# VectorE takes over GpSimd's arithmetic in a fused S5, GLU and mixture-of-experts layer, and TensorE takes eight modulation rows

## The chip, the cores and the metric

One core of a Trainium2 chip runs one launch of the kernel. The metric is the device time in microseconds, the median of several runs. Engines are named as in the profile: PE is TensorE, DVE is VectorE, ACT is ScalarE, POOL is GpSimd, SP is the engine that issues the transfers.

## The reference

One trunk layer on 1024 latent tokens and 256 context tokens of width 1024, in float32. What matters here, cut down:

```
c -> silu -> w_ada -> shift, scale, gate rows for both sub-layers      (modulation)
h = layer_norm(x) * (1 + scale) + shift
proj = h @ w_in  -> u_a, z_b, gate_b, gate_c, merge_a, merge_b
S5:    32 groups of 16 channels, 64 complex states, forward and backward
       s[t] = ab * s[t-1] + bb @ u[t];  y = Re(c @ s) + d * u
       context first, latent scans start from its final states; then GLU
conv:  conv3(gate_c * z), gated by gate_b, then conv_w_out
mix = (sigmoid(merge_a) * a + sigmoid(merge_b) * b) @ w_o
x1 = layer_norm(ALPHA * x + gate * mix);  h2 = modulate(layer_norm(x1))
router: top-1 expert group of 4, top-2 of its 8 experts; SwiGLU experts
out = layer_norm(ALPHA * x1 + gate2 * moe(h2))
```

## The kernel before, in words

A float32 product runs on TensorE in three passes: each operand is split in a rounded "hi" (ACT, `L91`) and a remainder "lo" (a subtraction, `L92`, on DVE or POOL), and hi·hi, lo·hi and hi·lo are summed in PSUM (`L95`, `L96`, `L97`). The whole program is one stream for each engine in the order in which the Python code emits it; nothing is reordered afterwards. The pieces are interleaved by hand with generators.

Until 129 us the modulation rows of the first sub-layer, the layer norm and the product that gives u are made. **Preparation** (to 290 us) then runs 20 "half units": `half()` issues the eight three-pass products (24 matmuls, tiles `g` from `hh`, `hl`, `wh`, `wl`) of one half of a weight unit of `w_in`; a unit is loaded two ahead (`load_unit`, tile `raw`) and its weight split one ahead (`split_unit`, tiles `wh`, `wl` of 128x1024, `L92` on POOL). The lists `before[h]` and `after[h]` say which piece of the S5 tables is made around half h: for each of four quarters q, `prep_v` makes complex products on DVE (`cmul`, `L692` to `L697`, six operations of 128x512), transposes and splits them; `prep_r` makes two more `cmul`, direction 0 on DVE and direction 1 on POOL, copies `bb` into `bpd` (`L722`), multiplies on PE (`L743`) and splits into `rh`, `rl`, half of it on POOL; `prep_m` makes the last tables. Every second half, `ada_slot` moves the remaining 32 modulation rows on by one stage: load the row's weights (`raw<-in_w_ada`), then on DVE `acc` = the sum over eight blocks of weight times the conditioning scalar (`L780` once, `L782` seven times), then on PE one matmul with a column of ones (`L788`) and on DVE an addition into `mr` (`L790`). One filler of dummy matmuls (`warm`, `L101`) stands in q = 3.

The **in-loop** (to 385 us) runs j from -2 to 15 over 16 pairs of groups: `in_a` transposes u (`L854`) and splits it on DVE (`ul`), `in_b` multiplies (12 matmuls into tiles `t`) and copies the results out of PSUM (`L875` on ACT, `L876` and `L877` on DVE), `in_c` transposes back (`L885`, `L887`) and copies to the scan's buffers (`L895`). A `half()` stands ahead of `in_b` at each odd j, an `ada_slot` at the end of each even j. The **scan** (to 528 us) is 160 steps on DVE (`L901`, `L904`); beside it PE runs the remaining halves, and 19.1 us of filler until the read-out. The read-out follows to 614, then the **GLU** to 752: for each of eight row blocks m, `glu_split` splits the weights on POOL, and `glu_post` multiplies the sigmoid in (`L1069`, POOL) and merges on DVE (`L1070` to `L1072`). The weight w_o (tiles `OW`, eight of 128x1024) is scaled by the gate row g2, three on POOL inside the GLU (`L1167`), five after it (`L1190`), and split with `wo_hi` (ACT) and `wo_lo` (`L1197`, DVE and POOL in turn). The **w_o product** runs in eight tiles of 128 tokens; between the tiles' products `stage_a` forms ALPHA·x + product (`L1451`), `stage_b` normalizes and modulates to `h` (`affine`, a DVE, an ACT and a POOL operation, `L1395`, `L1399`, `L1400`), `stage_c` transposes `h` (`L1504`) and runs the router. `stage_ab(7)` does the same for the last tile. Routing ends at 912 us; the experts take the rest.

Of the kernel before, what the change touches and what calls it, by code (L numbers as in the profile page):

```python
# [49 lines left out]
def block_kernel(ctx: ExitStack, tc: tile.TileContext, I, out):  # L50
# [598 lines left out]
    def half(before=(), after=()):  # L649
# [5 lines left out]
        if n == 0:  # L655
            split_unit(i + 1)
# [24 lines left out]
    def cmul(eng, n, q, tab, d, lo, a, b, c_, d_, op_re, op_im):  # L681
# [9 lines left out]
        x, y = (sb(sp, f"c{n}{z}", full) for z in "xy")  # L691
# [8 lines left out]
    def prep_v(q, d):  # L700
# [71 lines left out]
    def ada_rest(q):  # L772
# [6 lines left out]
        acc = sb(AR["pl"], "acc", [P, P])  # L779
        V.tensor_scalar(acc, w[:, 0, :], sc[:, 0, 0:1], None, op0=ALU.mult)  # L780
        for k in range(1, NK):
            V.scalar_tensor_tensor(acc, w[:, k, :], sc[:, k, 0:1], acc, op0=ALU.mult, op1=ALU.add)  # L782
# [5 lines left out]
        PE.matmul(pb[0:1, 0:P], ones, acc, start=True, stop=True)  # L788
# [27 lines left out]
    for q in range(4):  # L816
# [92 lines left out]
    for j in range(-2, NPAIR):  # L909
# [7 lines left out]
        if j % 2 and j < NPAIR - 1:  # L917
# [25 lines left out]
    while hstep[0] < 49:  # L943
        half([steps(8)])
# [28 lines left out]
    def ro_b(pr):  # L973
# [3 lines left out]
        warm(py, {0: 19.1, 12: 1.3, 13: 4.0, 15: 0.85}.get(pr, 0))  # L977
# [58 lines left out]
    def glu_split(m, xs=(1, 2, 0), eng=G):  # L1036
# [27 lines left out]
    def glu_post(m, n):  # L1064
# [4 lines left out]
        G.tensor_tensor(sgm, sgm, sga, op=ALU.mult)  # L1069
# [69 lines left out]
    ld(g2, mod_d[0].partition_broadcast(P))  # L1139
# [4 lines left out]
    for m in range(NK):  # L1144
# [5 lines left out]
        for n in range(2):  # L1150
# [54 lines left out]
    wo_hi(3)
    wo_scale(4, G)
    wo_hi(4)
    wo_scale(5, V)
    wo_scale(6, G)
    wo_lo(3, V)  # L1210
    wo_hi(5)
    wo_lo(4, G)
    wo_scale(7, V)
    wo_hi(6)
    wo_lo(5, V)
    wo_hi(7)
    wo_lo(6, G)
    wo_lo(7, V)
# [7 lines left out]
    G.memset(xgs[0], 0.0)  # L1226
# [218 lines left out]
    def stage_a(i, fill=()):  # L1445
# [14 lines left out]
    def stage_b(i, fill=()):  # L1460
# [4 lines left out]
        if i < 6:  # L1465
            affine(h2, x1, *o, bc["sc2"], bc["sh2"], G)
# [563 lines left out]
```

## Time and profile before

| | |
|---|---|
| runs shown | 1692.76, 1698.22, 1701.19 us, median 1698.22 |
| profiled execution | 1694.1 us, span 1692.3 us (1.8 us around it) |
| mean granted TensorE clock | 0.987 |
| busy: PE, DVE, ACT, POOL | 1577.4 (93%), 1347.9 (80%), 729.9 (43%), 495.3 us (29%) |

Busy shares say little by themselves, since the stages have different limits: they are read by stage, with the waits of the engine that has almost no idle time there. A "busy" PE includes dummy matmuls and matmuls at the lower clock.

### The profile page before, as it was taken

The page shows a single profiled execution, that of the slowest core. Times are in us where ns is not written, and L with a number is a line of the kernel's source. Part 1 is how long each engine was busy: PE and PEld are TensorE (multiplying, and loading weights), DVE is VectorE, ACT ScalarE, POOL GpSimd, SP SyncE. Part 2 cuts the span into 40 slices and gives each one's busy share as a digit, 9 for nine tenths or more (in the row PEclk, how much of TensorE's full clock was granted, in tenths as well). Part 3 has the DMA queues.
Part 4 walks back from the last instruction along what each step waited for, and adds up shares of the span by engine and source line. Part 5 has one row for each costly group of instructions (what it writes and reads, how often), then busy time and mean ns, then how long its engine had stood idle before and what let it go on. Part 6 is the DMA issues. An engine that isn't in the chain of part 4 may idle for free.

```text
span 1692.3 us, 23483 instructions
## 1 busy us (share of the span) xinstructions
PE 1577.4 (93%) x7594; PEld 1243.1 (73%) x7594; DVE 1347.9 (80%) x2871; ACT 729.9 (43%) x1059; POOL 495.3 (29%) x366
## 2 busy tenths in 40 slices
PE   7899899999998999988998999999999999999984
PEld 3688777888887777766876777777777777777751
DVE  7757987669999548987687695999995999686878
ACT  1443322442212352222222574777764777555632
POOL 1436562012222423444333120121221222120127
PEclk9999999999999999999999999999999999999998
DMA  8415767862322565554544595899995999776872
GB/s 318 160 55 185 215 193 238 275 209 101 100 81 78 157 190 180 192 165 160 185 174 136 192 363 199 327 362 356 373 339 195 353 356 373 288 264 238 292 303 100
DMA packets 141732, 381.62 MB, mean 226 GB/s; under 512 B 17632, under 2 KB 76160, under 8 KB 116992
## 3 DMA queue, kind: packets, MB, share of 16 engines
q1 hardware_dynamic: 130912, 362.80, 61.4%
q0 software_dynamic: 10656, 16.80, 2.7%
q8 instruction: 83, 1.36, 0.3%
q14 instruction: 81, 0.66, 0.1%
HBM read 336.98 MB, written 68.76 MB: 240 GB/s over the span
## 4 chain that ended last, share of the span: by engine, by line
issue 25%; DMA 24%; DVE 23%; PE 18%; POOL 4%; ACT 2%; SPq 2%; POOLq 1%; another core or an unknown queue 1%; DVEq 0%; ACTq 0%
DMA y_d<-yt,tbi 11%; DMA xo<-h_d,tbi 8%; DVE vs L904 4%; DVE sa L901 3%; DVE acc L782 3%; PE g L95 2%; PE g L97 2%; PE g L96 2%; DVE vc L904 1%; PE pu L95 1%; PE pu L97 1%; PE pu L96 1%; DMA raw<-in_w_ada 1%; PE misc L1511 1%; POOL h L1400 1%
## 5 line engine op out<-in xcount | busy, mean ns | idle before, releaser
L92 DVE TENSOR_TENSOR lo<-raw,hi 128x1024 fp32r<-128x1024 f32 x376 | 440.8, 1220 | 30.9 <-ACT hi L91 20.2
L91 ACT ACTIVATE hi<-raw 128x1024 fp32r<-128x1024 f32 x376 | 371.7, 1050 | 33.7 <-PEq L1871 20.5
L1728 POOL DMA_INDIRECT y_d<-yt,tbi x37 | 92.2, 2493 | 381.2 <-DVE yt L1721 300.0
L95 PE MATMUL g<-hh,wh 128*128 128x512 f32 x448 | 178.5, 398 | 0.0
L96 PE MATMUL g<-hl,wh 128*128 128x512 f32 x448 | 175.6, 392 | 0.0
L97 PE MATMUL g<-hh,wl 128*128 128x512 f32 x448 | 175.5, 392 | 0.0
L92 POOL TENSOR_TENSOR wl<-raw,wh 128x1024 fp32r<-128x1024 f32 x27 | 66.4, 2458 | 203.1 <-ACT wh L91 203.1
L95 PE MATMUL y<-hi,hh 128*128 128x512 f32 x256 | 102.5, 400 | 6.1 <-PEq L1871 2.1
L95 PE MATMUL g<-hi,xh 128*128 128x512 f32 x256 | 102.1, 399 | 4.2 <-issue 0.3
L95 PE MATMUL u<-hi,xh 128*128 128x512 f32 x256 | 105.8, 413 | 0.0
L97 PE MATMUL g<-hi,xl 128*128 128x512 f32 x256 | 100.6, 393 | 1.2 <-DVE xl L92 1.2
L97 PE MATMUL u<-hi,xl 128*128 128x512 f32 x256 | 100.9, 394 | 0.0
L96 PE MATMUL y<-lo,hh 128*128 128x512 f32 x256 | 100.6, 393 | 0.0
L96 PE MATMUL g<-lo,xh 128*128 128x512 f32 x256 | 100.6, 393 | 0.0
L97 PE MATMUL y<-hi,hl 128*128 128x512 f32 x256 | 100.2, 391 | 0.0
L96 PE MATMUL u<-lo,xh 128*128 128x512 f32 x256 | 99.9, 390 | 0.0
L95 PEld LDWEIGHTS g<-hh,wh 128*128 128x128 f32 x448 | 84.9, 189 | 19.4 <-issue 2.5
L97 PEld LDWEIGHTS g<-hh,wl 128*128 128x128 f32 x448 | 84.7, 189 | 18.3
L91 ACT ACTIVATE xh<-tp 128x512 fp32r<-128x512 f32 x64 | 37.5, 587 | 138.9 <-PE tp L1688 138.9
L96 PEld LDWEIGHTS g<-hl,wh 128*128 128x128 f32 x448 | 84.9, 189 | 16.9
L1566 POOL DMA_INDIRECT xg<-h_d,tbi x32 | 34.0, 1061 | 208.3 <-PE tp L1688 160.7
L610 ACT ACTIVATE sg<-g 128x512 f32<-128x512 f32 x32 | 19.1, 598 | 141.6 <-PE g L97 109.2
(508 smaller groups left out, 3759.0 us busy)
## 6 DMA issues: line engine op xcount, KB each, us to landing
raw<-in_w_exp SPq DMA_DIRECT2D x192, 1024.0 KB
raw<-in_w_r SPq DMA_DIRECT2D x28, 512.0 KB
w<-w_d SPq DMA_DIRECT2D x32, 384.0 KB
raw<-in_w_ada SPq DMA_DIRECT2D x20, 512.0 KB
sig_d<-sg SPq DMA_DIRECT2D x32, 256.0 KB
rp<-r_d SPq DMA_DIRECT2D x64, 128.0 KB
raw<-in_w_ada SPq DMA_DIRECT2D x6, 1024.0 KB
aw<-in_w_ada SPq DMA_DIRECT2D x12, 512.0 KB
```

Of the source, the lines that this page charges most:

```text
L91: S.activation(hi, src, AF.Copy)
L92: (eng or V).tensor_tensor(lo, src, hi.bitcast(F32), op=ALU.subtract)
L95: PE.matmul(ps, a[0], b[0], start=first, stop=False)
L96: PE.matmul(ps, a[0], b[1], start=False, stop=False)
L97: PE.matmul(ps, a[1], b[0], start=False, stop=last)
L610: S.activation(sg, pg, AF.Sigmoid)
L782: V.scalar_tensor_tensor(acc, w[:, k, :], sc[:, k, 0:1], acc, op0=ALU.mult, op1=ALU.add)
L901: V.tensor_tensor(t[d], cur[:, d].unsqueeze(2).to_broadcast([P, 2, 2, NPAIR]), kc[:, d], op=ALU.mult)
L904: V.tensor_tensor(new[:, d], new[:, d], t[d][:, r], op=ALU.add)
L1400: G.tensor_tensor(dst, dst, bias, op=ALU.add)
L1566: G.indirect_dma_start(out=xg, out_offset=None, in_=h2_d, in_offset=bass.IndirectOffsetOnAxis(ap=tbi[:, b, seq[e], 0:1], axis=0), bounds_c ...
L1728: G.indirect_dma_start(out=y_d, out_offset=bass.IndirectOffsetOnAxis(ap=tbi[:, b, seq[e], 1:2], axis=0), in_=yt, in_offset=None, bounds_ch ...
```

## The change

- In preparation, the `cmul` of direction 1, the `bpd` copies, the second half of the `rl` splits and (while fewer than 20 halves have been issued) the weight unit's `wl` split run on DVE instead of POOL. The two directions' `cmul` use one shared scratch pair, `rh` and `rl` have a buffer for each direction, and direction 1 comes one half later. The filler at q = 3 goes.
- The first eight of the 32 remaining modulation rows are no longer summed on DVE: eight float32 matmuls on PE take the conditioning column as the stationary operand and the weights as the moving one (`L792` of the new file).
- The in-loop carries five halves (j = -1, 2, 6, 9, 12) instead of eight; the other three run beside the scan. A half is put after each 7 scan steps instead of 8. The filler before the read-out shrinks from 19.1 to 1.7 us, and one of 1.3 us is added at read-out 9, one in the layer norm and one ahead of `stage_c1(6)`.
- `glu_split` and the sigmoid's product run on DVE.
- w_o is no longer scaled by the gate; its splits are all on DVE, in order. The gate row is loaded into `xgs[0]` and multiplied into the product (`tensor_mul`, 128x512, twice a tile) in `stage_a` and `stage_ab`; the second layer norm's `affine` of tiles 0 to 5 is two DVE operations.

```diff
...
-            split_unit(i + 1)
+            split_unit(i + 1, V if hstep[0] < HP else G)
...
-        x, y = (sb(sp, f"c{n}{z}", full) for z in "xy")
+        x, y = (sb(sp, f"c{z}", full) for z in "xy")
...
-            if (q, d, r) == (3, 1, 0):
-                warm(pt.rearrange("p a b -> p (a b)"), 8.5)
...
-                (G if d else V).tensor_copy(bpd[d][64 * h:64 * h + 64, :, :, 16 * h:16 * h + 16], bb[64 * h:64 * h + 64, :, d, sl])
+                V.tensor_copy(bpd[d][64 * h:64 * h + 64, :, :, 16 * h:16 * h + 16], bb[64 * h:64 * h + 64, :, d, sl])
...
-            rr.append(cmul(G if d else V, d, q, tab, d, lo, cr, ci, ni, cr, ALU.subtract, ALU.subtract))
+            if d:
+                yield
+            rr.append(cmul(V, d, q, tab, d, lo, cr, ci, ni, cr, ALU.subtract, ALU.subtract))
...
-            rh, rl = (sb(sk, f"r{x}", [P, QN, 2, P], F32R) for x in "hl")
+            rh, rl = (sb(sk, f"r{x}{d}", [P, QN, 2, P], F32R) for x in "hl")
             for r in range(2):
-                split(rh[:, :, r], rl[:, :, r], rr[d][r].rearrange("p q a b -> p q (a b)"), G if r else V)
+                split(rh[:, :, r], rl[:, :, r], rr[d][r].rearrange("p q a b -> p q (a b)"))
...
+        whole = q < 8
+        if not whole:
...
+        if whole:
+            for k in range(NK):
+                PE.matmul(pb[0:1, 0:P], sc[:, k, 0:1], w[:, k, :], start=(k == 0), stop=(k == NK - 1))
+        else:
+            PE.matmul(pb[0:1, 0:P], ones, acc, start=True, stop=True)
...
         before[b + 2].append(r)
+        before[b + 3].append(r)
...
-        if j % 2 and j < NPAIR - 1:
+        if j in (-1, 2, 6, 9, 12):
             half()
...
-        half([steps(8)])
+        half([steps(7)])
...
-        warm(py, {0: 19.1, 12: 1.3, 13: 4.0, 15: 0.85}.get(pr, 0))
+        warm(py, {0: 1.7, 9: 1.3, 12: 1.3, 13: 4.0, 15: 0.85}.get(pr, 0))
...
-    def glu_split(m, xs=(1, 2, 0), eng=G):
+    def glu_split(m, xs=(1, 2, 0), eng=V):
...
-        G.tensor_tensor(sgm, sgm, sga, op=ALU.mult)
+        V.tensor_mul(sgm, sgm, sga)
...
-            if m == 5 and n or m == 6:
-                i = 2 * m + n - 11
-                G.tensor_tensor(OW[i], OW[i], g2, op=ALU.mult)
...
-    for i in range(3):
+    for i in range(NK):
         wo_hi(i)
-    wo_lo(0, V)
-    wo_lo(1, G)
-    wo_lo(2, V)
-    wo_scale(3, V)
...
+        wo_lo(i, V)
...
-    G.memset(xgs[0], 0.0)
+    ld(xgs[0], mod_d[0].partition_broadcast(P))
...
-            V.scalar_tensor_tensor(tt[:, c], xa[n], ALPHA, pm[n], op0=ALU.mult, op1=ALU.add)
+            V.tensor_mul(tt[:, c], pm[n], xgs[0][:, c])
+            V.scalar_tensor_tensor(tt[:, c], xa[n], ALPHA, tt[:, c], op0=ALU.mult, op1=ALU.add)
...
-            affine(h2, x1, *o, bc["sc2"], bc["sh2"], G)
+            affine(h2, x1, *o, bc["sc2"], bc["sh2"], V)
...
+    G.memset(xgs[0], 0.0)
...
```

Three places show how the order on an engine moves. The first is DVE in preparation, between the end of one quarter's `prep_r` multiplication and the next quarter's (`c0`, `cx` and `c1` are `cmul` tiles, `pd` and `pa` power tables, `scm` and `ncim` the C matrix, `svl`, `rl`, `wl` remainders); before:

```order
L92 TENSOR_TENSOR svl<-t,svh 128x8x64 x2
L739 TENSOR_TENSOR kk<-dd,t 32x4x16
L92 TENSOR_TENSOR rl<-c0r,rh 128x4x128
L692 TENSOR_TENSOR c0r<-pd,bb 128x512
L693 TENSOR_TENSOR c0x<-pd,bb 128x512
```

and of the change at the same place:

```order
L92 TENSOR_TENSOR svl<-t,svh 128x8x64 x2
L692 TENSOR_TENSOR c1r<-pd,scm 128x512
L693 TENSOR_TENSOR cx<-pd,scm 128x512
L694 TENSOR_TENSOR c1i<-pd,ncim 128x512
L695 TENSOR_TENSOR cy<-pd,scm 128x512
L696 TENSOR_TENSOR c1r<-c1r,cx 128x512
L697 TENSOR_TENSOR c1i<-c1i,cy 128x512
L739 TENSOR_TENSOR kk<-dd,t 32x4x16
L92 TENSOR_TENSOR rl_1598<-c0r,rh_1597 128x4x128
L92 TENSOR_TENSOR rl_1598<-c0i,rh_1597 128x4x128
L92 TENSOR_TENSOR wl<-raw,wh 128x1024
L692 TENSOR_TENSOR c0r<-pd,bb 128x512
```

Six operations of direction 1, the second `rl` split and the unit's `wl` split have come into DVE's queue.

The second is PE in the in-loop, at the end of an even j and the start of an odd one; before, where a half stands between `in_a` and `in_b`:

```order
L885 MATMUL t<-ident,vj 128x128 x4
L887 MATMUL t<-ident,vjc 128x32 x4
L788 MATMUL t<-acc,ones 1x128
L854 MATMUL t<-ident,uj 128x128 x2
L95 MATMUL g_3152<-hh,wh 128x512
L96 MATMUL g_3152<-hl,wh 128x512
L97 MATMUL g_3152<-hh,wl 128x512
```

and of the change, where the same lines are numbered `L892`, `L894`, `L794` and `L861`:

```order
L892 MATMUL t<-ident,vj 128x128 x4
L894 MATMUL t<-ident,vjc 128x32 x4
L794 MATMUL t<-acc,ones 1x128
L861 MATMUL t<-ident,uj 128x128 x2
L95 MATMUL t<-w,uh 128x384
L96 MATMUL t<-w,uh 128x384
L97 MATMUL t<-w,ul 128x384
```

The 24 matmuls of the half are gone, so `in_b` follows the transposes at once; DVE's order there (`mr`, `acc` and its seven additions, `ul`, `uj` twice, `vjc`) is the same in both.

The third is DVE between the last but one and the last block of the GLU, where w_o is made ready; before:

```order
L1197 TENSOR_TENSOR lo<-hi 128x1024 x2
L1190 TENSOR_TENSOR lo<-lo,g2b 128x1024 x2
L1197 TENSOR_TENSOR lo<-lo,hi 128x1024
L1190 TENSOR_TENSOR tt<-tt,g2b 128x1024
L1197 TENSOR_TENSOR lo<-lo,hi 128x1024
L1197 TENSOR_TENSOR lo<-tt,hi 128x1024
L1070 TENSOR_TENSOR sgb<-po,sgb 128x512
```

and of the change:

```order
L1197 TENSOR_TENSOR lo<-hi 128x1024 x3
L1197 TENSOR_TENSOR lo<-lo,hi 128x1024 x4
L1197 TENSOR_TENSOR lo<-tt,hi 128x1024
L1076 TENSOR_TENSOR sgm<-sgm,sga 128x512
L1077 TENSOR_TENSOR sgb<-po,sgb 128x512
```

The scalings are gone, all eight remainders are here, and the sigmoid's product has come in behind them.

## Rows read from the trace of the kernel before

**Rows 1.** Windows: stretch, length, busy PE PEld DVE ACT POOL (count), PE clock, DMA, GB/s.

```profile
129.20:289.90 160.70, 150.29 (x854) 122.74 (x853) 136.26 (x195) 45.34 (x69) 84.70 (x55) 0.98 0.67 202
289.90:385.00 95.10, 94.56 (x562) 77.96 (x560) 59.16 (x160) 42.59 (x92) 9.79 (x4) 1.00 0.72 238
385.00:528.00 143.00, 143.00 (x636) 119.33 (x636) 142.74 (x970) 23.09 (x33) 30.05 (x13) 1.00 0.26 86
...
614.00:752.00 138.00, 133.26 (x580) 104.98 (x579) 111.01 (x220) 38.28 (x104) 55.59 (x40) 0.99 0.50 168
752.00:782.00 30.00, 24.65 (x106) 19.20 (x104) 24.55 (x34) 7.08 (x11) 17.83 (x11) 1.00 0.50 172
782.00:865.00 83.00, 77.79 (x419) 64.94 (x418) 54.11 (x110) 17.65 (x26) 33.74 (x24) 1.00 0.57 193
```

**Rows 2.** PE's waits in preparation: tile and line, releaser, total us, times, longest.

```profile
PE t L788 <- DVE svl L92: 6.0, 1, 6.0
```

**Rows 3.** Timeline of DVE in preparation: start us, duration us, what, [idle before].

```profile
226.71 2.88 DVE L692 TENSOR_TENSOR c0r<-pd,bb 128x512 f32<-128x512 f32 x1
229.51 0.68 DVE L693 TENSOR_TENSOR c0x<-pd,bb 128x512 f32<-128x512 f32 x1
```

**Rows 4.** Timeline of POOL, in preparation and around the w_o split.

```profile
226.20 2.83 POOL L92 TENSOR_TENSOR wl<-raw,wh 128x1024 fp32r<-128x1024 f32 x1
...
730.94 2.39 POOL L1167 TENSOR_TENSOR hi<-hi,g2b 128x1024 f32<-128x1024 f32 x1
...
753.00 6.70 POOL L1190 TENSOR_TENSOR lo<-lo,g2b 128x1024 f32<-128x1024 f32 x2
```

**Rows 5.** DVE's groups in preparation, by form: count, busy us, mean ns, idle before.

```profile
L782 DVE SCALAR_TENSOR_TENSOR acc<-raw,sc,acc 128x128 f32<-128x128 f32 x49 | 28.8, 589 | 1.7
```

**Rows 6.** Timeline of PE: a row's matmul in preparation, and an in-loop iteration.

```profile
230.52 0.38 PE L788 MATMUL t<-acc,ones 128*1 128x128 f32 x2
230.83 0.50 PE L95 MATMUL g<-hh,wh 128*128 128x512 f32 x1
...
325.31 0.44 PE L854 MATMUL t<-ident,uj 128*128 128x128 f32 x2
...
331.07 0.34 PE L95 MATMUL t<-w,uh 128*128 128x384 f32 x1
...
332.82 0.60 PE L885 MATMUL t<-ident,vj 128*128 128x128 f32 x4
```

**Rows 7.** PE's filler in preparation, by form: count, busy us, mean ns, idle before.

```profile
L101 PE MATMUL t<-ident 128*128 128x256 f32 x40 | 8.8, 379 | 0.0
```

**Rows 8.** Timeline of DVE in the in-loop and at the scan's start.

```profile
325.93 2.68 DVE L782 SCALAR_TENSOR_TENSOR acc<-raw,sc,acc 128x128 f32<-128x128 f32 x7
328.53 0.42 DVE L92 TENSOR_TENSOR ul<-t,uh 128x256 fp32r<-128x256 f32 x1
...
384.62 4.69 DVE L782 SCALAR_TENSOR_TENSOR acc<-raw,sc,acc 128x128 f32<-128x128 f32 x7
```

**Rows 9.** Timeline of the scan, all engines.

```profile
418.20 0.35 DVE L901 TENSOR_TENSOR sa<-vs,kc 128x64 f32<-128x64 f32 x2
...
418.92 0.35 DVE L901 TENSOR_TENSOR sa<-vs,kc 128x64 f32<-128x64 f32 x2
...
419.61 2.39 POOL L92 TENSOR_TENSOR wl<-raw,wh 128x1024 fp32r<-128x1024 f32 x1 [8.43 <-ACT wh L91]
419.64 2.56 DVE L901 TENSOR_TENSOR sa<-vs,kc 128x64 f32<-128x64 f32 x2
```

**Rows 10.** DVE in the GLU, timeline.

```profile
729.87 5.55 DVE L782 SCALAR_TENSOR_TENSOR acc<-aw,sc,acc 128x128 f32<-128x128 f32 x7
```

**Rows 11.** PE's waits from 752 to 912 us.

```profile
PE tp L1504 <- POOL h L1400: 5.2, 6, 2.3
PE pm L96 <- DVE lo L1197: 2.9, 2, 2.2
PE pm L96 <- POOL lo L1197: 2.4, 2, 1.7
```

More of the change, by code (lines that the diff above doesn't have):

```diff
@@ L374, in ln_p @@
                 TP[x, q] = sb(ps1, "tp", [P, 4, P], bufs=3)
-                if q == 0 and x in (0, 2):
-                    warm(TP[x, q].rearrange("p a b -> p (a b)"), 2.1 if x else 0.85)
+                if q == 0 and x in (0, 2, 5):
+                    warm(TP[x, q].rearrange("p a b -> p (a b)"), (0.85, 0, 2.1, 0, 0, 1.3)[x])
                 for z in range(4):
@@ L778, in ada_rest @@
             ld(BR[q // 2][0], I["b_ada"][0:1, 2048 + q * P:2048 + (q + 2) * P])
[L779 to L782, printed above, removed]
+        whole = q < 8
+        if not whole:
+            acc = sb(AR["pl"], "acc", [P, P])
+            V.tensor_scalar(acc, w[:, 0, :], sc[:, 0, 0:1], None, op0=ALU.mult)
+            for k in range(1, NK):
+                V.scalar_tensor_tensor(acc, w[:, k, :], sc[:, k, 0:1], acc, op0=ALU.mult, op1=ALU.add)
         yield
@@ L787, in ada_rest @@
         pb = sb(pst, "t", [P, 512])
-        PE.matmul(pb[0:1, 0:P], ones, acc, start=True, stop=True)
+        if whole:
[3 more added lines that the diff above has]
+            PE.matmul(pb[0:1, 0:P], ones, acc, start=True, stop=True)
         c = slice((q % 2) * P, (q % 2 + 1) * P)
@@ L1138, in block_kernel @@
     MG = [sb(bigp, "raw", [P, 2, NK, P], F32R) for _ in range(NT)]
-    ld(g2, mod_d[0].partition_broadcast(P))
     hia = pool(ctx, "hia", 3)
@@ L1187, in block_kernel @@
     WO = [None] * NK
-    def wo_scale(i, eng):
-        eng.tensor_tensor(OW[i], OW[i], g2, op=ALU.mult)
     def wo_hi(i):
@@ L1197, in wo_lo @@
         eng.tensor_tensor(WO[i][1], OW[i], WO[i][0].bitcast(F32), op=ALU.subtract)
-    for i in range(3):
+    for i in range(NK):
         wo_hi(i)
-    wo_lo(0, V)
-    wo_lo(1, G)
-    wo_lo(2, V)
-    wo_scale(3, V)
[L1205 to L1218, printed above, removed]
+        wo_lo(i, V)
     glu_post(7, 1)
@@ L1478, in stage_ab @@
             c = slice(n * 512, (n + 1) * 512)
-            V.scalar_tensor_tensor(tt[:, c], xa[n], ALPHA, pm[n], op0=ALU.mult, op1=ALU.add)
+            V.tensor_mul(tt[:, c], pm[n], xgs[0][:, c])
+            V.scalar_tensor_tensor(tt[:, c], xa[n], ALPHA, tt[:, c], op0=ALU.mult, op1=ALU.add)
             V.bn_stats(st[:, n, :], tt[:, c])
@@ L1618, in block_kernel @@
     dma_w()
+    WB.append(sb(psb, "pm0", [P, 512]))
+    warm(WB[0], 1.3)
     stage_c1(6)
     stage_c2(6)
-    WB.append(sb(psb, "pm0", [P, 512]))
     warm(WB[0], 5.5)
     stage_ab(7, fill)
+    G.memset(xgs[0], 0.0)
     stage_c1(7)
```

## The prediction

> **What bounds the kernel now.** I read the windows by stage first, then TensorE's waits in each stage, then the timelines at those waits. In every stage that the change touches TensorE has almost no idle time: 10.4 us of 160.7 in preparation, 0.5 of 95.1 in the in-loop, none of 143 in the scan, 4.7 of 138 in the GLU, and 5.4 + 5.2 = 10.6 from 752 to 865 us [rows 1]. So a stage is as long as TensorE's own work plus its idle time, and only what changes one of these counts. The scan is the exception: VectorE is busy 142.7 of 143 us there, and TensorE is kept full with spare halves and filler.
>
> The idle time comes from instructions of other engines. The longest wait of preparation is 6.0 us for a VectorE remainder [rows 2]. VectorE is slow there: one and the same 128x512 multiplication takes 2.88 us where a GpSimd split started just before it, and the next one takes 0.68 [rows 3, 4]. The seven additions of a modulation row cost 2.68 us in one in-loop iteration and 4.69 in another [rows 8]; in preparation they average 0.589 us each, against 2.68/7 = 0.383 [rows 5, 8]. In the scan, a pair of VectorE's small operations goes from 0.35 to 2.56 us at the moment at which a 2.39 us split starts on GpSimd [rows 9]. I conclude that a long GpSimd instruction takes VectorE's time nearly one for one while it lasts, and that GpSimd needs about twice as long for the same tile: 2.39 us for 128x1024, against 2 x 0.68 = 1.36.
>
> [...]
>
> **Preparation.** VectorE: 28.8 us of additions leave [rows 5]; what comes, at 0.68 for 128x512, is 24 multiplications (16.3), 4 remainders (2.7), 10 unit splits at 1.36 (13.6) and 8 small copies (at most 2.7), 35.3 in all. From 136.3 [rows 1] this gives 142.8 even if nothing gets faster. Contention also leaves: the long multiplication alone is 2.2 us over its short form [rows 3], once in each of ten units makes 22. So VectorE needs 121 to 143 us, with something over 150 to do it in, and it is no longer late by much.
> TensorE: 150.3 busy [rows 1], minus 8.8 of filler [rows 7]. A whole row adds seven matmuls to the one that stands there; the one takes 230.83 - 230.52 = 0.31 us in two passes [rows 6], of which 0.09 is the change of operand, so a matmul is 0.22 and a row 7 x 0.22 = 1.53 dearer. Six rows are in preparation: +9.2. Idle time does not go to zero, since transposes still wait on VectorE's products: I leave 2.5 of the 10.4 (bounds 0 and 10.4). New length: 150.3 - 8.8 + 9.2 + 2.5 = 153.2, that is **-7.5** (bounds -10.0 and +0.4).
> A row's weights now stay in their buffer until TensorE has read them, one slot later than before, and a unit's load behind them on the transfer queue goes out about one half (5.6 us) later. Units are loaded two ahead, so I cost it at nothing; without that cover it is a wait up to 5.6 for each of six rows (the third rival).
>
> **In-loop.** A half is 331.07 - 325.51 = 5.56 us (the transposes at 325.31 take 0.20) [rows 6]; three fewer: -16.7. Two whole rows: +3.1. The 0.5 of idle time goes. Then a new wait. At the start of an odd j VectorE still has the row's additions (2.68), the remainder ul (0.42) and the copy uj (0.29) in its queue, and TensorE's transposes at the end of the iteration need the PSUM buffer that this copy empties. With the half between, TensorE got there 5.56 us later and waited for nothing. Without it, `in_b` takes 332.82 - 331.07 = 1.75, so TensorE is there at 325.51 + 1.75 = 327.26; the copy ends at 328.53 + 0.40 + 0.29 = 329.22 [rows 6, 8] and hands over some 0.1 later: 2.05 of wait. This falls on the odd iterations that follow a summed row and have no half: j = 3, 5, 7, 11, 13, so +10.3 (bounds 0 and 12). Sum -16.7 + 3.1 - 0.5 + 10.3 = **-3.8** (bounds -14.1 and -2.1).
>
> **Scan.** It starts when VectorE has done the last row's additions, 4.69 us beside a GpSimd split, 2.68 without [rows 8]: **-2.0**. The three halves that have moved here bring two more GpSimd splits than before, 2.56 - 0.35 = 2.2 each [rows 9]: **+4.4**. TensorE's 26 halves take 26 x 5.5 = 143, so the shorter filler about fills the rest; a few us of idle time may lower its clock at the read-out's start: **+1.4**, the middle between 0 and 2.8 (half of a half unit's 5.56, if its first half ran at half speed).
>
> **GLU.** The 4.7 us of idle time are one wait [rows 1]: VectorE's merge stands behind additions of 5.55 us [rows 10], during which GpSimd runs a scaling of 2.39 us [rows 4]. The scaling is gone: **-4.7** (bounds 0 and -4.7). VectorE takes 24 splits and 16 products of 0.68 more, 27 us on 111 of 138: it would be full if nothing got faster, but the 55.6 us of GpSimd work beside it go.
>
> **w_o and its product.** Two scalings of 6.70 us together leave GpSimd [rows 4], and the eight remainders on VectorE are 8 x 1.36 = 10.9 us, less than TensorE needs for eight blocks of a tile (13.7 with all its terms). The waits for remainders, 2.9 and 2.4, and the six for h, 5.2 [rows 11], were what TensorE's 10.6 us of idle time consisted of. VectorE gets 2 x 0.68 for the gate and one more 128x1024 operation a tile, some 2.7 us of 13.7, with 54 of 83 us busy before [rows 1]; h no longer passes through three engines. **-10.0** (bounds -5 and -10.6). For the last tile nothing hides the two gate products: **+1.3**.
>
> The other fillers lie in stalls that exist and are costed at nothing. Sum: -7.5 - 3.8 - 2.0 + 4.4 + 1.4 - 4.7 - 10.0 + 1.3 = **-20.9**. From the profiled 1694.1 us this is **1673.2**. That run lies 4 us below the median of the runs shown (1698.2) and inside their spread of 8.4.
>
> **Rivals.**
> *The in-loop does not wait.* If the transposes' PSUM buffer is free in time, the 10.3 us stay gained: 1673.2 - 10.3 = 1662.9. For it: TensorE has no wait there now. Against it: the order of VectorE's queue there is unchanged, and the arithmetic above leaves 2 us. Chance 0.17.
> *Preparation keeps its length.* VectorE's products come late, or unit loads do, and TensorE's idle time and the filler's cover stay while the rows come on top: between 0 and +9.2 in place of -7.5, 1680.7 to 1689.9. For it: every edit here lengthens a queue of work in which TensorE waits for the last link. Against it: 121 us in 150. Chance 0.16.
> *Slower: VectorE was not slowed by GpSimd.* If its long instructions have another cause, they stay long and the moved ones are long too. At the 1.5 times of 0.589 against 0.383, the 35.3 us become 53 and VectorE has 160 in preparation, with 10 of waits as now: +10 in place of -7.5; the GLU's 27 become 41, 152 in a stage of 138: +14 in place of -4.7; the w_o gain is lost. 1673.2 + 17.5 + 18.7 + 10 = 1719. It decides when the moved 128x512 operations average above about 1.0 us. Against it stand the pairs of rows in which only GpSimd's presence differs. Chance 0.04.
> *Given back to the experts.* The stages from the GLU on are shortened, and the first expert weights could then be late: up to 13.4 (4.7 + 10.0 - 1.3) returns, 1686.6. Against it: transfers are at half their time there (0.50 to 0.57) [rows 1]. Chance 0.08.
>
> **How the numbers follow.** The forecast itself has 0.55, in 1661 to 1684. The range 1655 to 1690 takes in the first, second and last rival and leaves out the slower one and the edges, about 0.15. A change of under 0.5% (8.5 us) can't be told from none by the runs. Faster by more than that is below 1689.7: 0.86; within it 0.10 (the ends of the second and last rival); slower 0.04.
>
> **What would show it.** Preparation near 153 us with no GpSimd splits in it and 128x512 operations at 0.68; in-loop near 91 with five waits of 2 us of the `vj` transposes for the `uj` copy; the scan 2 longer, twelve blocks of 2.2 in it; GLU near 133; 752 to 865 us without waits for remainders or h. It would be wrong if preparation kept a wait for a VectorE product in every quarter, or if the in-loop lost no time at the transposes.

## The result, and the profile after

The changed kernel takes 1672.32 us (median of 4 runs, 1670.58 to 1674.46), the kernel before 1695.49 in the same comparison (1692.07 to 1701.19): ratio 0.9861, 95% interval 0.9827 to 0.9894. The forecast was 1673.2 in a range of 1655 to 1690. The profiled execution is the slowest of the four, 1674.46 us with a span of 1672.6; against the profiled one of before the span is 19.7 shorter.

The windows of the changed kernel follow, cut at the same events as those of before: preparation, in-loop, scan, read-out, GLU, w_o product, tail (to the experts' first transposes), experts. The columns are those of [rows 1].

```profile
127.60:276.00 148.40, 148.40 (x897) 121.18 (x896) 112.53 (x189) 45.38 (x69) 3.31 (x5) 1.00 0.74 225
276.00:368.70 92.70, 85.31 (x517) 69.30 (x515) 49.10 (x152) 39.89 (x88) 7.18 (x3) 0.96 0.65 217
368.70:514.10 145.40, 143.47 (x634) 118.60 (x632) 145.12 (x971) 26.03 (x37) 32.70 (x14) 1.00 0.28 93
514.10:603.80 89.70, 77.68 (x414) 64.81 (x415) 55.03 (x97) 37.28 (x58) 32.53 (x31) 0.92 0.63 168
603.80:739.00 135.20, 135.20 (x597) 107.20 (x596) 108.39 (x260) 43.35 (x109) 0.44 (x2) 1.00 0.52 172
739.00:843.50 104.50, 103.33 (x536) 87.36 (x535) 87.18 (x177) 15.04 (x29) 25.01 (x21) 1.00 0.57 206
843.50:889.80 46.30, 37.69 (x218) 31.07 (x216) 35.85 (x144) 12.04 (x19) 9.19 (x10) 0.89 0.20 70
889.80:1672.00 782.20, 725.31 (x3202) 559.18 (x3202) 636.51 (x683) 461.27 (x541) 173.57 (x98) 0.98 0.79 292
```

The kernel before, cut at the same events (the GLU to the first w_o matmul, the product to its last, so that the cuts differ from those of [rows 1]):

```profile
129.20:290.20 161.00, 150.59 (x857) 123.04 (x856) 136.26 (x195) 45.49 (x70) 84.70 (x55) 0.98 0.67 202
290.20:384.90 94.70, 94.16 (x559) 77.60 (x557) 59.08 (x160) 42.34 (x92) 9.79 (x4) 1.00 0.72 238
384.90:527.80 142.90, 142.90 (x637) 119.22 (x636) 142.62 (x971) 23.19 (x33) 30.05 (x13) 1.00 0.26 86
527.80:614.10 86.30, 74.89 (x418) 62.37 (x417) 53.35 (x96) 37.17 (x58) 33.51 (x32) 0.98 0.62 171
614.10:755.90 141.80, 137.06 (x596) 108.26 (x595) 114.81 (x221) 38.18 (x104) 59.49 (x41) 0.99 0.51 169
755.90:872.10 116.20, 105.64 (x536) 86.42 (x534) 81.56 (x159) 25.74 (x39) 49.23 (x35) 1.00 0.53 181
872.10:911.70 39.60, 34.66 (x211) 28.92 (x210) 33.12 (x140) 11.92 (x19) 8.66 (x9) 0.91 0.23 81
911.70:1692.00 780.30, 723.83 (x3202) 558.33 (x3202) 637.29 (x685) 460.91 (x541) 173.86 (x99) 0.99 0.79 292
```

Three stages have become shorter where that was meant: preparation by 12.2 (before, it ends at 289.85, so the cut at 290.20 gives it 0.35 too much), the GLU by 6.6, the w_o product by 11.7; TensorE is busy for the whole of preparation and of the GLU. Two have become longer where nothing was meant to: the read-out by 3.4, at a lower granted clock (0.92, before 0.98), and the tail by 6.7, at about the same mean clock (0.89, before 0.91) but with the slow stretch in another place, as shown below. The experts, 1.9 longer here, took 778 to 785 us in the runs below, so nothing is read from that; nor from the start of preparation, which lay between 127.5 and 132.5.

What was slow on VectorE is slow no longer. Its groups in preparation, by form, with count, busy us and mean ns:

```profile
L92 DVE TENSOR_TENSOR wl<-raw,wh 128x1024 fp32r<-128x1024 f32 x10 | 13.2, 1320 | 3.1 <-ACT wh L91 2.7
L692 DVE TENSOR_TENSOR c0r<-pd,bb 128x512 f32<-128x512 f32 x4 | 2.7, 680 | 0.0
L720 DVE COPY bp<-bb 64x128 f32<-64x128 f32 x16 | 3.5, 219 | 0.2
```

The multiplication that took 2.88 us in [rows 3] averages 0.68, and the unit's split 1.32.

The new wait of the in-loop is there. TensorE's waits from 300 to 620 us (releaser, us in total, times, longest), and one of them in the timelines of TensorE and VectorE:

```profile
PE t L892 <- DVE uj L883: 6.9, 5, 1.7
PE t L95 <- DMA rp<-r_d: 5.8, 4, 2.2
PE t L95 <- issue: 4.9, 1, 4.9
```

```profile
360.51 2.68 DVE L784 SCALAR_TENSOR_TENSOR acc<-raw,sc,acc 128x128 f32<-128x128 f32 x7
363.10 0.42 DVE L92 TENSOR_TENSOR ul<-t,uh 128x256 fp32r<-128x256 f32 x1
363.44 0.48 DVE L883 COPY uj<-t 128x128 f32<-128x128 f32 x2
...
363.77 0.66 PE L892 MATMUL t<-ident,vj 128*128 128x128 f32 x4 [1.31 <-DVE uj L883]
```

The transposes start when the first copy behind the seven additions ends, five times. The 4.9 us under "issue" are TensorE's idle time ahead of the read-out.

### The profile page after: what moved, and what is told of

Same layout as the page of the kernel before. It is cut to its first block, busy times and chain, and to the rows that moved or that the text cites. A ratio compares the mean times of both kernels' runs of the same rounds, so it can differ in the third digit from the quotient of the medians.

```text
span 1672.6 us, 23420 instructions
## 1 busy us (share of the span) xinstructions
PE 1570.5 (94%) x7602; PEld 1237.4 (74%) x7602; DVE 1320.1 (79%) x2917; ACT 725.3 (43%) x1053; POOL 330.5 (20%) x264
## 4 chain that ended last, share of the span: by engine, by line
PE 34%; DMA 24%; issue 21%; DVE 17%; POOL 1%; SPq 1%; POOLq 1%; another core or an unknown queue 0%; ACT 0%; DVEq 0%; ACTq 0%
DMA y_d<-yt,tbi 13%; DMA xo<-h_d,tbi 8%; DVE vs L911 4%; DVE sa L908 4%; PE g L95 3%; PE g L97 3%; PE g L96 3%; PE t L97 2%; PE t L95 2%; PE t L96 2%; PE pm L95 1%; DVE vc L911 1%; PE pm L96 1%; PE pm L97 1%; DVE acc L784 1%
## 5 line engine op out<-in xcount | busy, mean ns | idle before, releaser
L1715 POOL DMA_INDIRECT y_d<-yt,tbi x37 | 92.3, 2495 | 382.0 <-DVE yt L1708 300.4
L92 POOL TENSOR_TENSOR wl<-raw,wh 128x1024 fp32r<-128x1024 f32 x17 | 41.1, 2419 | 330.8 <-ACT wh L91 330.8
L95 PEld LDWEIGHTS g<-hh,wh 128*128 128x128 f32 x448 | 84.3, 188 | 19.1 <-issue 2.3
L96 PEld LDWEIGHTS g<-hl,wh 128*128 128x128 f32 x448 | 84.3, 188 | 16.7
```

The lines of the kernel that those rows point to most:

```text
L92: (eng or V).tensor_tensor(lo, src, hi.bitcast(F32), op=ALU.subtract)
L95: PE.matmul(ps, a[0], b[0], start=first, stop=False)
L96: PE.matmul(ps, a[0], b[1], start=False, stop=False)
L1715: G.indirect_dma_start(out=y_d, out_offset=bass.IndirectOffsetOnAxis(ap=tbi[:, b, seq[e], 1:2], axis=0), in_=yt, in_offset=None, bounds_ch ...
```

## The experiments

Single runs are read by stage, between the same events as above. Preparation, in-loop, scan stage (to the last scan step), read-out, GLU, w_o product and tail, in us, with the steps' own time in brackets:

| run | prep. | in-loop | scan stage | read-out | GLU | w_o | tail | time |
|---|---|---|---|---|---|---|---|---|
| before | 160.6 | 95.1 | 142.9 (138.3) | 86.3 | 141.8 | 116.2 | 39.6 | 1694.1 |
| changed | 148.4 | 92.7 | 145.4 (142.9) | 89.7 | 135.2 | 104.5 | 46.2 | 1674.5 |
| e1_prep_gpsimd | 152.8 | 91.1 | 145.2 (142.6) | 88.2 | 135.2 | 104.5 | 46.2 | 1675.2 |
| e2_rows_dve | 144.5 | 93.4 | 145.1 (142.6) | 85.1 | 135.2 | 104.5 | 45.5 | 1669.6 |
| e3_halves_back | 148.4 | 97.2 | 142.8 (138.2) | 85.7 | 135.2 | 104.5 | 46.0 | 1672.9 |
| e4_scan_dve | 148.4 | 91.3 | 132.1 (128.7) | 92.2 | 135.2 | 104.5 | 46.1 | 1662.4 |
| e5_glu_wo_gpsimd | 148.4 | 92.7 | 145.5 (142.9) | 91.0 | 135.2 | 115.7 | 45.3 | 1681.4 |
| e6_tail_filler | 148.4 | 91.1 | 145.5 (142.9) | 88.8 | 135.2 | 104.5 | 45.1 | 1670.8 |
| e7_all | 144.5 | 99.0 | 133.0 (129.6) | 84.1 | 135.2 | 104.5 | 41.8 | 1651.9 |
| e8_memset | 148.4 | 91.3 | 131.8 (129.2) | 92.6 | 135.2 | 104.5 | 46.2 | 1663.4 |
| e9_prep_both_back | 160.7 | 91.7 | 145.5 (142.9) | 91.6 | 135.2 | 104.5 | 45.1 | 1690.3 |
| e10_rows_inloop | 148.4 | 89.4 | 143.3 (142.9) | 87.4 | 135.2 | 104.5 | 46.0 | 1663.5 |
| e11_one_r | 148.4 | 91.3 | 145.5 (142.9) | 90.5 | 135.2 | 104.5 | 45.4 | 1677.2 |
| e12_one_r_rows_dve | 148.3 | 92.3 | 145.5 (142.9) | 88.2 | 135.2 | 104.6 | 46.2 | 1672.6 |

Stages without an edit repeat to 0.1 us in preparation, GLU and w_o product, the scan's steps to 0.3, the tail to about 1.1 (45.1 to 46.2), the in-loop to 1.6 (91.1 to 92.7), the read-out to 2.8 (88.2 to 91.0), and the total also has the scatter of its start and of the experts.

**e1_prep_gpsimd, e2_rows_dve, e9_prep_both_back: the two edits of preparation undone, one at a time and together.**

```diff
-            split_unit(i + 1, V if hstep[0] < HP else G)
+            split_unit(i + 1)
...
-            rr.append(cmul(V, d, q, tab, d, lo, cr, ci, ni, cr, ALU.subtract, ALU.subtract))
+            rr.append(cmul(G if d else V, d, q, tab, d, lo, cr, ci, ni, cr, ALU.subtract, ALU.subtract))
...
-            rh, rl = (sb(sk, f"r{x}{d}", [P, QN, 2, P], F32R) for x in "hl")
+            rh, rl = (sb(sk, f"r{x}", [P, QN, 2, P], F32R) for x in "hl")
```

(e1, with the copies, the scratch and the second r split as before too; e2 has `whole = q < 0` alone; e9 has both.)

> The changed kernel, with GpSimd's arithmetic of preparation put back (unit splits, direction 1's complex product and its scratch, copies, half of the r splits, one r buffer); the rows stay on TensorE and the filler stays out. Changed kernel: preparation 148.4 us, no wait of TensorE in it. Theory (VectorE is slowed by GpSimd's long instructions): 128x512 operations of VectorE average over 0.8 us again and TensorE's waits come back, preparation 153 to 160, the rest as in the changed kernel. Rival (taking the rows' additions off VectorE was enough): VectorE has the time to spare, preparation stays within 1.5 us of 148.4 though GpSimd is busy 60 us in it.

> The changed kernel with all 32 modulation rows summed on VectorE, as before. Theory: TensorE loses 9.2 us of work in preparation and VectorE gets 20 more on 112 of 148, at 2.95 a row undisturbed by GpSimd; the waits that come back are below 5 us, so preparation is 140 to 145 and the rows on TensorE were not needed for the gain. Two more rows are summed in the in-loop, so it has one or two more waits of 1.4 us and 3.1 us less matmul work. Rival (the rows on TensorE are what freed preparation): waits of 9 us or more return and preparation is 148 or longer.

> The changed kernel with both edits of preparation undone, GpSimd's arithmetic back and all rows summed on VectorE; only the filler stays out and direction 1 stays one half later. So far preparation was 148.4 us with both edits, 152.8 with GpSimd back alone, 144.5 with the rows back alone, 160.6 in the kernel before; TensorE's own work is 139.3 without the rows. Theory (each alone leaves VectorE enough time, both together don't): 152 to 158, with 13 us or more of waits and VectorE over 128 us busy. Rival (the filler and the step's place were all that mattered): 144 to 149.

With GpSimd back, 152.8: just below the theory's range and well above the rival's. VectorE is held up again (the multiplications average 0.93 us, in the changed kernel 0.68), but without the rows it has time to spare, and 2.9 us of TensorE's waits for `svl` are most of what comes back. With the rows back and GpSimd out, 144.5, as the theory had it: the rows on TensorE cost 3.9 us of preparation. With both back, 160.7, above the theory's 152 to 158 and what the kernel before had. So either edit would have done most of it, and the second one of them, the rows, costs more than it saves once the first is made. TensorE's waits in e9's preparation, and VectorE's timeline ahead of the longer one:

```profile
PE t L709 <- DVE c0r L696: 10.2, 1, 10.2
PE t L794 <- DVE svl L92: 6.0, 1, 6.0
```

```profile
227.13 2.88 DVE L692 TENSOR_TENSOR c0r<-pd,bb 128x512 f32<-128x512 f32 x1
...
238.67 0.69 DVE L92 TENSOR_TENSOR rl<-c1r,rh 128x512 fp32r<-128x512 f32 x1 [5.66 <-DMA r_d<-rl]
...
240.64 6.81 DVE L784 SCALAR_TENSOR_TENSOR acc<-raw,sc,acc 128x128 f32<-128x128 f32 x7
247.37 1.54 DVE L692 TENSOR_TENSOR c0r<-pa,bb 128x512 f32<-128x512 f32 x1
```

The 10.2 us stand where the filler stood [rows 7], from 243 to 254 us: that filler lay in a wait, and taking it out bought nothing. VectorE's queue shows three causes in a row: a transfer that empties the r buffer, additions of 6.81 instead of 2.68 beside GpSimd's split, copies and first multiplications, and multiplications of 1.5 to 1.75 instead of 0.68 beside GpSimd's.

**e11_one_r, e12_one_r_rows_dve: is it the r buffer or GpSimd?** The edit is the third of the diff above, alone and with the rows on VectorE.

> The changed kernel with one buffer for rh and rl instead of one for each direction; nothing else. In the runs with one buffer VectorE's rl and ScalarE's rh stood 8 to 11 us behind the transfer that empties it; with two there was no such wait. Theory A (the buffer mattered by itself): the wait of VectorE for that transfer comes back in two quarters and TensorE's preparation is 150 to 154 instead of 148.4. Theory B (VectorE has the slack for it as long as GpSimd leaves it alone): the wait comes back but preparation stays within 1 us of 148.4.

> One buffer for rh and rl, and all rows summed on VectorE; GpSimd stays out of preparation. With two buffers this was 144.5, with one buffer and GpSimd's work back 160.7. Theory A (buffer): 152 to 158, so that most of the 16 us between the two is the transfer's. Theory B (GpSimd): 144.5 to 149.

With the rows on TensorE one buffer costs nothing (148.4), though VectorE waits 7.0 us for its transfer. With the rows on VectorE it costs 3.8 (144.5 to 148.3), and GpSimd's arithmetic then 12.4 more (160.7). Theory B holds in both; the buffer is the smaller part.

**e3_halves_back: the three halves.**

```diff
-        if j in (-1, 2, 6, 9, 12):
+        if j % 2 and j < NPAIR - 1:
...
-        half([steps(7)])
+        half([steps(8)])
...
-        warm(py, {0: 1.7, 9: 1.3, 12: 1.3, 13: 4.0, 15: 0.85}.get(pr, 0))
+        warm(py, {0: 19.1, 9: 1.3, 12: 1.3, 13: 4.0, 15: 0.85}.get(pr, 0))
```

> The changed kernel with eight halves at the odd j of the in-loop, a half for each 8 scan steps and the 19.1 us of filler. Theory: the five waits of the transposes for the uj copy and the low clock beside them vanish; the in-loop grows from 92.7 to 99 (16.7 of halves, minus 6.9 of waits, minus some 3 of slow matmuls), the scan shrinks by two GpSimd splits (4.4) and the read-out by 2 to 3 (its clock is full at its start): in all 0 to 2 us faster or slower than the changed kernel, so that moving the three halves bought nothing. Rival (the waits come from elsewhere): in-loop 109, the total 7 to 10 slower.

The in-loop has no wait and is full (97.2 us busy of 97.2), 4.5 longer; the scan stage is 2.6 and the read-out 4.0 shorter. In sum 2.1 less than in the changed kernel, in the total 1.5 less, both within the scatter: moving the halves bought nothing that can be seen, as the theory had it.

**e10_rows_inloop: the in-loop's wait, from its other end.** `whole = q < 15`, so that no row is summed on VectorE there.

> The changed kernel with fifteen rows instead of eight as matmuls on TensorE, so that no row is summed on VectorE in the in-loop. Theory (the transposes wait for the uj copy because seven additions stand ahead of it in VectorE's queue): the five waits of 1.4 to 1.7 vanish and the clock stays full; the in-loop gets six whole rows of 1.53 (9.2) and loses 6.9 of waits and some 3 of slow matmuls, 91 to 93; the scan starts 2 us earlier against the in-loop's end, so the scan stage is 143.4 instead of 145.4. Rival (the copy is late because of what TensorE or ScalarE give it): the waits stay and the in-loop is 100 or longer.

No wait is left and TensorE is busy 92.0 of 92.0 us in the stretch; the in-loop is 89.4 and the scan stage 143.3. In the in-loop, the rows on TensorE do pay, 1.7 to 3.3 us there (against 91.1 to 92.7 in runs without the edit) and 2.1 in the scan stage: there the additions stood ahead of a copy that TensorE waits for. The total is 11 us less, but 4.7 of it are the experts' scatter.

**e4_scan_dve and e8_memset: what a split on GpSimd costs the scan.** The edit makes the last lines of `split_unit` return VectorE's subtraction, which `half` issues behind the scan steps (the in-loop's three splits go to VectorE too, without the delay):

```diff
-            split_unit(i + 1, V if hstep[0] < HP else G)
+            late_lo = split_unit(i + 1, V, hstep[0] > HP + 5)
         for f in before:
             next(f, None)
+        if n == 0 and late_lo:
+            late_lo()
```

e8 adds `G.memset(lo.bitcast(F32), 0.0)` ahead of it.

> The changed kernel with the remaining weight splits (in-loop and scan) on VectorE too, in the scan behind the steps of a half. Theory (GpSimd's split blocks VectorE for 2.2 us, the split on VectorE itself takes 1.2 to 1.3): the scan's 160 steps go from 142.9 to about 132, TensorE's halves become the bound there, the read-out starts 5 to 7 us earlier and at a higher clock: 6 to 9 us faster. Rival (the split's time is the same wherever it runs, or VectorE has to wait for ScalarE's hi part): the scan stays at 142 to 150.

> The scan splits on VectorE, and beside them GpSimd writes zeros into each unit's remainder tile (128x1024) ahead of VectorE's split, so that GpSimd writes SBUF and reads none of it; the zeros are overwritten. Theory A (any long GpSimd instruction holds VectorE up): a pair of VectorE's small operations beside each 1 us memset takes about 1 us instead of 0.35, and the scan is 10 to 12 us longer than 128.7. Theory B (only one that reads SBUF does): pairs stay at 0.35, the scan within 1 us of 128.7.

The steps take 128.7 instead of 142.9 us, 14.2 less. Twelve stalls of 2.2 are gone, and eleven splits have come in, each of which delays the next step by 1.14 (381.76 to 382.90 below); the twelfth starts at 500.26 and stands behind the last step. That is 26.4 - 12.5 = 13.9, the theory's prices. VectorE's timeline in e4, and its group of splits in the scan, by form:

```profile
381.31 0.54 DVE L918 TENSOR_TENSOR vc<-vc,sa 128x32 f32<-128x32 f32 x4
381.76 1.22 DVE L466 TENSOR_TENSOR wl<-raw,wh 128x1024 fp32r<-128x1024 f32 x1
382.90 0.35 DVE L915 TENSOR_TENSOR sa<-vc,kc 128x64 f32<-128x64 f32 x2
```

```profile
L466 DVE TENSOR_TENSOR wl<-raw,wh 128x1024 fp32r<-128x1024 f32 x12 | 14.7, 1224 | 0.0
```

The split waits for nothing. TensorE's halves now run beyond the last scan step, into the read-out, so 10.8 us of the 14.2 arrive in scan stage and read-out together. With the memset the steps take 129.2, and beside it VectorE keeps its pace (GpSimd's timeline, then VectorE's, in e8):

```profile
374.80 0.95 POOL L466 MEMSET wl<- 128x1024 f32 x1 [242.18 <-DVE sa L916]
...
375.14 0.36 DVE L916 TENSOR_TENSOR sa<-vc,kc 128x64 f32<-128x64 f32 x2
```

So theory B's numbers: the twelve memsets cost 0.5 us in all. It is not any work of GpSimd that slows VectorE. Nor is it the length alone. The changed kernel has two longer memsets beside its scan, 1.8 us each, and the steps there keep their pace as well:

```profile
498.16 3.56 POOL L960 MEMSET rp<- 128x2048 f32 x2
...
499.52 0.36 DVE L908 TENSOR_TENSOR sa<-vs,kc 128x64 f32<-128x64 f32 x2
```

That it is the reading of SBUF that makes the difference is not shown by this: no run has two GpSimd instructions that differ in nothing else.

**e5_glu_wo_gpsimd: GpSimd's work of GLU and w_o put back.**

```diff
-    def glu_split(m, xs=(1, 2, 0), eng=V):
+    def glu_split(m, xs=(1, 2, 0), eng=G):
...
-        V.tensor_mul(sgm, sgm, sga)
+        G.tensor_tensor(sgm, sgm, sga, op=ALU.mult)
...
-        wo_lo(i, V)
+        wo_lo(i, G if i % 2 else V)
...
-            affine(h2, x1, *o, bc["sc2"], bc["sh2"], V)
+            affine(h2, x1, *o, bc["sc2"], bc["sh2"], G)
```

> The changed kernel with GpSimd's work of the GLU and of w_o put back, each in its own stage: GLU splits and the sigmoid's product on GpSimd, every second w_o remainder on GpSimd, the last step of the affine of tiles 0 to 5 on ScalarE and GpSimd; w_o stays unscaled and the gate stays on the product. Changed kernel: GLU 135.2 us with no wait, w_o product 104.5. Theory: the GLU's 4.7 us came from the scalings that GpSimd did beside a modulation row, and they are still gone: GLU within 1 us of 135.2 though the split and product groups on GpSimd take 45 us. In the w_o product the remainders on GpSimd (2.4 to 2.8 each, VectorE's beside them lengthened) and h bring back 2 to 5 us. Rival (VectorE taking the splits is what freed the GLU): GLU 139 or longer, w_o 110 or longer.

The GLU does not notice 47 us of GpSimd work (135.2), as the theory had it: its gain is the scaling's, by elimination and by the additions ahead of the merge, which take 3.59 us beside GpSimd's splits and products and took 5.55 with a scaling as well [rows 10]:

```profile
717.08 3.59 DVE L784 SCALAR_TENSOR_TENSOR acc<-aw,sc,acc 128x128 f32<-128x128 f32 x7
```

The w_o product gets 11.2 us longer, more than the theory's 2 to 5 and what the rival named, nearly all that it had gained. TensorE's waits in it, and VectorE's and GpSimd's timelines ahead of it:

```profile
PE tp L1489 <- POOL h L1383: 8.3, 6, 3.7
```

```profile
735.99 2.52 DVE L1197 TENSOR_TENSOR lo<-hi 128x1024 fp32r<-128x1024 f32 x1 [0.83 <-ACT hi L1194]
...
737.39 3.36 POOL L1197 TENSOR_TENSOR lo<-lo,hi 128x1024 fp32r<-128x1024 f32 x1
```

Side by side the two engines need 4.8 us for two remainders (735.99 to 740.75), where VectorE alone needs 2 x 1.22. But no matmul waits for a remainder: the 5.3 us of such waits before [rows 11] went with the scalings. What comes back is h, through three engines again, 8.3 us of waits; TensorE's busy time is 4.1 longer as well, at a granted clock of 0.97.

**e6_tail_filler: the tail.** `warm(WB[0], 5.5)` becomes `warm(WB[0], 10.2)`.

> The changed kernel with the filler ahead of the last tile's layer norm 10.2 us instead of 5.5. There TensorE idles 4.7 us and then runs the last transposes, router matmuls and fillers at the lower clock (granted 0.57 from 858 to 870 us), and the stretch from the last w_o matmul to the experts' first transposes is 46.25 us against 39.62 before. Theory (the lost clock is what lengthened it, beside the 1.3 us of two gate products): 41 to 42 us, 4 to 5 faster in all. Rival (the stretch is VectorE's chain, longer by other waits): 45 to 46.5, nothing gained.

45.1: of the 4 to 5 us expected, 1.1, and that is no more than the scatter, since e9, without an edit there, also has 45.1. The windows of the tail, of the changed kernel and then of e6:

```profile
843.50:857.00 13.50, 10.22 (x57) 8.45 (x55) 12.81 (x27) 4.15 (x7) 3.11 (x4) 1.00 0.43 155
857.00:869.00 12.00, 9.80 (x38) 8.52 (x39) 6.13 (x23) 4.43 (x7) 1.88 (x2) 0.61 0.12 45
```

```profile
842.00:856.00 14.00, 13.00 (x56) 10.82 (x55) 13.31 (x27) 4.21 (x6) 3.55 (x5) 0.76 0.42 151
856.00:868.00 12.00, 11.69 (x73) 10.18 (x72) 6.52 (x32) 4.23 (x7) 0.97 (x2) 1.00 0.11 44
```

The low clock has moved: in the changed kernel it falls on the router and the fillers behind the idle time (0.61 from 857 to 869 us), in e6 on the filler itself (0.76 from 842 to 856), which then takes 13.2 us (from 847.09 to 860.33) instead of 10.4 and is what the transposes wait for. In e7 the same filler ran at the full clock (granted 1.00 from 828.3 to 870.1 us) and the tail took 41.8. So in these runs the place of the low clock goes with the tail's length (46.2, 45.1 and 41.8 us), and a filler of this length is no sure cure.

**e7_all: the parts put together.** Rows on VectorE, eight halves in the in-loop, e4's splits, 8.1 us of filler ahead of the read-out, 10.2 in the tail.

> The changed kernel with what the first runs showed put together: all modulation rows summed on VectorE, eight halves at the odd j, the splits of in-loop and scan on VectorE behind the steps, 8.1 us of filler ahead of the read-out, 10.2 ahead of the last layer norm. Theory: preparation 144.5, in-loop 94, scan stage 131 to 132, read-out 85, GLU 135, w_o 104.5, tail 41 to 42, rest 782: with the start at 128 to 130 that is 1645 to 1650 us. Rival (the parts do not add, since VectorE's new splits delay the read-out or the rows delay preparation): 1655 or more.

Median 1653.04 us of 4 runs (1650.33 to 1658.11), ratio to the kernel before 0.9742, interval 0.971 to 0.9774: 19 us faster than the changed kernel's median (timed in another comparison, where the ratio was 0.9861), between the theory's 1645 to 1650 and the rival's 1655. The in-loop is 5 us longer than reckoned, 2.8 of it TensorE's waits for the transfers `w<-w_d`.

## Why the prediction was right, step by step

**Preparation, -7.5: measured -12.2** (160.6 to 148.4), outside its own bounds of -10.0 to +0.4. Its cause, VectorE slowed by GpSimd, is shown: with the rows on VectorE and one r buffer, GpSimd's arithmetic is worth 12.4 us (e9 against e12). Two sizes were off. The 2.5 us of waits that I left in are zero, and busy time fell by 2.3 more than the rows and the filler explain. Some 1.3 of this can be read off the trace of before: behind the wait of 6.0 us the granted clock was 0.50 from 208 to 214 us, and the first matmuls there started 0.43 us apart instead of 0.23. The other 1.0 stays open.

```profile
211.43 0.58 PE L788 MATMUL t<-acc,ones 128*1 128x128 f32 x2 [5.97 <-DVE svl L92]
212.97 0.63 PE L97 MATMUL g<-hh,wl 128*128 128x512 f32 x1
213.40 0.63 PE L95 MATMUL g<-hh,wh 128*128 128x512 f32 x1
```

That the rows on TensorE cost 1.53 each was right (1.84 us in place of 0.31: in the trace of before the two-pass matmuls `L743` ahead of a row's start 0.22 us apart, and the product behind the row's starts 0.31 after it, 0.09 more), and so, as a cost, was +9.2; what I did not see is that by the other edit VectorE would have had time for them, so that the rows are a loss of 3.9 there. The unit loads' cover held. VectorE needed 112.5 us, less than my 121 to 143: the contention that left is worth 142.8 - 112.5 = 30.3, where I had 22.

**In-loop, -3.8: measured -2.4** (to -4.0 in the runs without an edit there, so the number itself stands within the scatter). The wait is there, in five iterations as named, 6.9 us where the sum had 10.3: TensorE comes some 0.5 later than I had it, 0.36 of it since `in_b` starts 0.56 instead of 0.20 us after the transposes, VectorE's ul and uj follow closer on each other, and the transposes start 0.04 after a copy of 0.29 (363.44 to 363.73, then 363.77) where I had some 0.1. Against that, TensorE's busy time is 85.3 us where the sum leaves 94.6 - 16.7 + 3.1 = 81.0, most of it by the clock (0.96 in the stage), which fell behind two of the five waits, to 0.70 from 305.4 to 311 us and to 0.73 from 328.6 to 335, and stayed at 1.00 behind the other three: the step left that out. e3 and e10 remove the wait from its two ends.

**Scan, -2.0 and +4.4: measured -2.0 and +4.5.** The steps start 2.5 instead of 4.6 us after the in-loop's end, and take 142.9 instead of 138.3, 2.27 for each of the two splits that came. e4 shows that the price is GpSimd's: the split itself takes VectorE 1.22.

**Read-out, +1.4: measured +3.4** (1.9 to 4.7 in the runs without an edit there). Right in kind, too small: TensorE idles 4.9 us ahead of it and runs at 0.55 of the full clock from 518 to 526.

```profile
510.00:518.00 8.00, 2.94 (x12) 2.03 (x11) 6.75 (x39) 2.65 (x4) 0.90 (x1) 0.81 0.02 8
518.00:526.00 8.00, 7.50 (x30) 6.31 (x31) 7.89 (x9) 4.15 (x7) 8.00 (x8) 0.55 0.31 76
```

**GLU, -4.7: measured -6.6.** The wait is gone, and by e5 it was the scaling's. The other 1.9 us are TensorE's busy time (137.06 to 135.20): before, the granted clock was 0.99 in the stage and 0.72 from 736 to 742 us, behind the wait of 4.7 that ends at 736.07; now it is 1.00 in the stage.

**w_o, -10.0: measured -11.7**, beyond its bound of -10.6. By e5 the waits for h were the work of the three engines; the waits for remainders went with the scalings, since GpSimd's remainders alone bring none. Idle time fell by 9.4, near the sum. The other 2.3 are busy time (105.64 to 103.33), which the sum had left as it was. The clock is not its cause, at 1.00 in both. An estimate for part of it: in the trace of before a matmul of the product takes 0.39 us and the next one usually starts 0.23 after it (870.98, 871.21, 871.44), so each of the ten waits [rows 11] also leaves 0.16 us of the matmul ahead of it uncovered, 1.6 in all. No run tests this.

**Tail, +1.3: measured +6.6.** From the last w_o matmul to the last tile's transposes it is 843.53 to 859.20, 15.7 us, against 872.1 to 886.45, 14.4, before: +1.3, as the sum had it, though in part by luck: VectorE's chain to the last h became 1.9 longer, and before, the transposes came some 0.6 after h, because the filler ahead of them ran at a low clock (0.68 from 878.15 to 886.45 us) and reached that far. The other 5.3 lie behind, where nothing was costed. TensorE's timeline, of the changed kernel from the filler on and then the same filler before:

```profile
848.82 5.86 PE L101 MATMUL pm<-ident 128*128 128x256 f32 x26
859.20 1.50 PE L1489 MATMUL tp<-ident,h 128*128 128x128 f32 x8 [4.51 <-DVE tmp L1315]
860.59 3.63 PE L1496 MATMUL misc<-rw,ht 128*128 128x36 f32 x16
864.03 3.76 PE L101 MATMUL pm<-ident 128*128 128x256 f32 x8
```

```profile
878.15 8.46 PE L101 MATMUL pm<-ident 128*128 128x256 f32 x26
```

Before, the router matmuls behind took 1.98 and their fillers 1.97. So both kernels have a stretch at a low granted clock, 0.68 from 878.15 to 886.45 us before and 0.53 from 859.20 to 868.00 now. Before, it lay on the filler, which took 8.46 us and left no idle time ahead of the transposes, so it cost next to nothing. Now the filler runs at the full clock (1.00 from 848.82 to 854.68), is done after 5.86, TensorE idles 4.5 us for h (the profile names the instruction behind it on VectorE), and the low clock falls behind that, on work that the experts wait for.

So the total was right partly because errors of both signs met: 8.3 us too little gain in preparation, GLU and w_o, 8.7 too much in in-loop, read-out and tail. The errors of the second kind have one thing in common, the clock behind a wait (0.70 and 0.73 in the in-loop, 0.55 in the read-out, 0.53 in the tail), which the sum had priced for the read-out alone; in the in-loop and the read-out they are no larger than the stage's own scatter.

**The rivals.** That the in-loop does not wait: no, five waits. That preparation keeps its length: no, though e9 shows what would have kept it; the late unit loads, which the prediction's text on preparation sends to the third rival, belong to this one, and did not come. That VectorE's long instructions have another cause than GpSimd: no, by e4 and by e9 against e12. That the time is given back to the experts: nothing beyond their scatter.

## What to carry to other kernels

Where two engines get in each other's way, moving the slower one's elementwise work to the faster one can shorten both (here a 128x1024 split of 2.39 us on GpSimd held the scan up by 2.2, and one of 1.22 on VectorE itself by 1.14): reckon the price by what the pair takes together, not by each engine's busy share. Two edits that relieve the same queue must be costed one after the other; here either was nearly enough, and the second one then cost 3.9 us. A removed wait was worth more than its idle time here (in the GLU 6.6 us for 4.7), and a new one cost more, where TensorE's clock fell behind it: in preparation (0.50), in-loop (0.70 and 0.73), read-out (0.55), GLU (0.72) and tail (0.53), though not behind three of the in-loop's five waits and not in the w_o product (1.00). Filler that stood in a wait was worth nothing by being taken out, and whether a filler itself ran at the low clock decided what stood behind it.

## What the runs showed of the hardware

I had not expected that GpSimd slows VectorE only with some of its instructions: in the scan, a subtraction of two 128x1024 tiles on GpSimd, 2.39 us long, takes 2.2 us of VectorE's time (2.56 instead of 0.35 for a pair of its small operations [rows 9]), a memset of 128x1024, 0.95 us long, next to none (pairs of 0.35 and 0.36 beside it in e8, 0.5 us over twelve), and so with the two memsets of 1.8 us each (a pair of 0.36 beside them). What it is in the two kinds that makes the difference, these runs do not show.
